# Two transformer blocks on one core: the factors for the down projection are made one by one between the next pair's products

## The chip, the core and the metric

The kernel runs on one core of a Trainium2 chip. The metric is the device time of one execution in microseconds (us). The time before is 2848.76 us, the median of 3 runs (2841.24 to 2850.15). The profile and the trace are from one further execution.

The engines are named as in the profile: PE is the matrix engine (PEld its weight loads), DVE the vector engine, ACT the scalar engine, POOL GpSimd, SP the engine that issues most loads. ACTq and SPq are the queues on which ACT and SP issue transfers.

## The reference, cut to what matters

The program runs two transformer blocks, one after the other, on 1024 tokens of width 1024. Each is a mixer (attention and others, not touched here) and a feed-forward part with 2816 hidden units:

```python
# block 1
gu = x @ w_gu                            # 1024x1024 @ 1024x5632
gate, up = gu[:, :2816], gu[:, 2816:]
ffn = (silu(gate) * up) @ w_down         # 1024x2816 @ 2816x1024
x = layer_norm(ALPHA * x + ffn, ln2_g, ln2_b)
# block 2: its six modulation rows depend on c alone
mod = silu(c) @ w_cond + b_cond          # 1x1024 @ 1024x6144
...
h = rmsnorm(x, g_ffn_pre) * (1 + scale_f) + shift_f
f = (silu(h @ w_gate) * (h @ w_up)) @ w_down
x = x + gate_f * rmsnorm(f, g_ffn_post)
```

All of it is float32. The kernel writes each factor of a matrix product as a high part (a cast to fp32r, in which PE takes it) and a low part (the rest), and makes three matmuls of each: high by high, high by low, low by high (`mm3`, L97 to L99).

## The kernel before, in words

The feed-forward part is the class `Ffn`, used once in each block (FFN1 and FFN2). Its first half, `gate_up`, has 22 tiles of 128 hidden units. Tiles 0 to 3 go through `direct`: 48 matmuls for the gate and 48 for the up part of one tile and one half of the tokens. Tiles 4 to 21 go in nine pairs p = 2 to 10. For a pair, gate and up are each a product of a 2x2 block matrix made with seven block products in place of eight (a Strassen scheme of Winograd's kind, class `Matrix`). Each block product is 12 matmuls of 128x512. The seven come in the order 1, 6, 2, 7, 5, 4, 3, first all of the gate, then all of the up part. The trace names a product by its right factor:

| product q | 1 | 6 | 2 | 7 | 5 | 4 | 3 |
|---|---|---|---|---|---|---|---|
| right factor | B11 | T2 | B21 | T3 | T1 | B12 | B22 |
| line of its eviction | 958 | 963 | 983/992 | 966 | 968 | 971 | 976 |

The weights of a product are one of four raw blocks or one of four sums of them (tile `tt`, DVE, L925). Their high part is an ACT cast (tile `wst`, L945); the low part is made on DVE, or on POOL for products 2 and 4 (L946). The results of a pair are four 128x512 blocks; the up part multiplies into the gate's on DVE (L992) or on POOL (L994).

When a pair is done, `forms` makes the left factors that the down projection will need: A11, S3, S2, A22, S1, A12, S4 for the pairs 0 to 8 (four of them are sums or differences made on DVE, L1042 to L1051). The pairs 9 and 10 have four plain stores each. `store` casts a factor on ACT (tile `hf`, L80), makes its low part on DVE (L84) and remembers it; the next `store` first issues what is remembered, from ACT's own queue (L1023), to DRAM (`h_d`, `hl_d`). `hf` and `wst` are slots of one tag, `w`, of which there are six: a cast into a slot that held an `hf` waits until its store has landed.

During FFN1's nine pairs `cond_steps` computes block 2's modulation rows: 48 loads of 512 KB (`raw_c`, three slots of the tag `raw`), each with one DVE operation on 128x1024 (L1250, L1252), and at the end of each of the six rows a split (L1264), two matmuls and a copy. One step is asked for after every second product (`extra1`). FFN2 has no such steps.

The program's text does not fix the order on the engines alone. A scheduler places each instruction by its dependencies and its priority; what stands in a `with soon():` block gets a high one. Each engine then takes its instructions strictly in the order that results.

Of the kernel before, what the change touches and what calls it, by code (L numbers as in the profile page):

```python
# [9 lines left out]
F32 = mybir.dt.float32  # L10
F32R = mybir.dt.float32r
# [12 lines left out]
P = 128  # L24
NB = S // P
KT = D // P
# [12 lines left out]
def two_blocks(ctx: ExitStack, tc: tile.TileContext, a):  # L39
# [16 lines left out]
    def slot(tag, shape, dtype, name):  # L56
        return strm.tile(shape, dtype, tag=tag, bufs=SLOTS[tag], name=name)
# [16 lines left out]
    def soon():  # L74
        return tc.high_priority(offset=4000)


    def split(hi, lo, src, hi_eng="act", lo_eng="dve"):
        if hi_eng == "act":
            A.copy(hi, src)  # L80
        else:
            V.tensor_copy(hi, src)
        eng = V if lo_eng == "dve" else G
        eng.tensor_tensor(lo, src, hi.bitcast(F32), op=OP.subtract)  # L84

    def load_split(src, shape, hi_eng="act", lo_eng="dve", alloc=slot):
        r = slot("raw", shape, F32, "raw")
        DMA.dma_start(r, src)
        h = alloc("w", shape, F32R, "wh")
        l = alloc("w", shape, F32R, "wl")  # L90
        with soon():
            split(h, l, r, hi_eng, lo_eng)
        return h, l
# [367 lines left out]
    for n, blk in enumerate(SCORED):  # L461
        if n % 4 == 0:
            iqt = p1.tile([P, 4, 256], F32, tag="qk", bufs=6, name="iq")
        o = gemm_tm(wiq, blk, 256)
# [134 lines left out]
    class LaneC:  # L599
# [7 lines left out]
        def load(self, j):  # L607
            return [load_qk(p1, 6, qk_d[4 + j], s) for s in range(2)]
# [168 lines left out]
    class SAct:  # L777
# [20 lines left out]
        def next(self):  # L798
            self.n += 1
            return self.ring[(self.n - 1) % len(self.ring)]  # L800
# [195 lines left out]
    class Ffn:  # L996
# [18 lines left out]
            DMA.dma_start(r, src)  # L1015
            return r

        def post(self, nm):
            return self.pp.tile([P, 512], F32, tag="post", bufs=12, name=nm)

        def flush(self):
            for dst, src in self.stores:
# [3 lines left out]
        def store(self, dst, x):  # L1026

            self.flush()
            t = slot("w", [P, 2, 512], F32R, "hf")
            split(t[:, 0], t[:, 1], x)  # L1030
            self.stores.append((dst, t.bitcast(F32)))

        def forms(self, i, b):

            if i >= NPAIR:
                for (j, th), x in b.items():
                    self.store(hl_d[2 * (i - NPAIR) + j][:, :, th * 512:(th + 1) * 512], x)
                return
            a11, a12, a21, a22 = b[0, 0], b[1, 0], b[0, 1], b[1, 1]
            put = lambda n, x: self.store(h_d[i][n], x)  # L1040
            s1 = self.post("s1")
            V.tensor_tensor(s1, a21, a22, op=OP.add)  # L1042
            put("A11", a11)
            V.tensor_tensor(a21, a11, a21, op=OP.subtract)  # L1044
            put("S3", a21)
            V.tensor_tensor(a11, s1, a11, op=OP.subtract)
            put("S2", a11)
            put("A22", a22)
            put("S1", s1)
            put("A12", a12)  # L1050
            V.tensor_tensor(a12, a12, a11, op=OP.subtract)  # L1051
            put("S4", a12)

        def gate_up(self, wg, wu, late, extra=None):


            act = self.act

            def direct(f, th, g, u):
                pg = ps_lg()  # L1060
                for n, (wh, wl) in enumerate((g, u)):
                    for k in range(KT):
                        mm3(pg[:, n, :], wh[:, k, :], wl[:, k, :], act.at(0, k, th), act.at(1, k, th), k == 0, k == KT - 1)
                s = self.post("silu")
                with soon():
                    A.activation(s, pg[:, 0, :], AF.Silu)
                    V.tensor_tensor(s, s, pg[:, 1, :], op=OP.mult)
                return s

            def load_gu(f):  # L1070
                return load_split(wg(f), [P, KT, P]), load_split(wu(f), [P, KT, P])

            wt = [self.w0, load_gu(1)]
            b = {}
            for th in range(2):
                for f in range(2):
                    b[f, th] = direct(f, th, *wt[f])
                    if th == 0:
                        late(4 + 2 * f)
                        late(5 + 2 * f)  # L1080
            self.forms(0, b)
            b = {}
            for f in (2, 3):
                wt = load_gu(f)
                for th in range(2):
                    b[f - 2, th] = direct(f, th, *wt)
            act.sums()
            self.forms(1, b)
            for p in range(2, NFT // 2):
                f = 2 * p  # L1090
                ms = {}
                for m in range(2):
                    w = (wg, wu)[m]
                    ms[m] = (Gate, Up)[m]([self.load(w(f + i), [P, KT, P]) for i in range(2)], act, self.post)
                    if m == 1:
                        ms[1].gate = ms[0]
                    for q in (1, 6, 2, 7, 5, 4, 3):
                        ms[m].product(q)
                        if extra is not None:
                            extra()  # L1100
                self.forms(p, {(i, l): ms[0].p[i, l] for i in range(2) for l in range(2)})
            self.flush()

        def down(self, wd, res=None):
# [138 lines left out]
    def cond_steps(j):  # L1243

        m = fpool.tile([P, D], F32, tag="rows", bufs=1, name="mod")
        for k in range(KT):
            r = slot("raw", [P, D], F32, "raw_c")
            DMA.dma_start(r, a["w_cond_2"][k * P:(k + 1) * P, j * D:(j + 1) * D])
            if k == 0:
                V.tensor_scalar_mul(m, r, sc[:, 0:1])  # L1250
            else:
                V.scalar_tensor_tensor(m, r, sc[:, k:k + 1], m, op0=OP.mult, op1=OP.add)  # L1252
            yield

        b = slot("raw", [P, D], F32, "raw_b")
        DMA.dma_start(b[0:1, :], a["b_cond_2"][j * D:(j + 1) * D].partition_broadcast(1))
        V.tensor_tensor(m[0:1, :], m[0:1, :], b[0:1, :], op=OP.add)
        gn = {1: "g_mix_pre_2", 2: "g_mix_post_2", 4: "g_ffn_pre_2", 5: "g_ffn_post_2"}.get(j)
        if gn is not None:
            g = row(slot("raw", [P, D], F32, "raw_g"), a[gn])  # L1260
        for c in range(2):
            cs = slice(c * 512, (c + 1) * 512)
            t = slot("raw", [P, 2, 512], F32, "raw_m").bitcast(F32R)
            split(t[:, 0, :], t[:, 1, :], m[:, cs])  # L1264
            o = ps_mm(512)
            T.matmul(o, ones, t[:, 0, :], start=True, stop=False)
            T.matmul(o, ones, t[:, 1, :], start=False, stop=True)
            V.tensor_copy(m[:, cs], o)
            yield
        if gn is not None:  # L1270
            V.scalar_tensor_tensor(m, m, 1.0 if j in (1, 4) else 0.0, g, op0=OP.add, op1=OP.mult)
        DMA.dma_start(mod_d[j:j + 1, :], m[0:1, :])
# [471 lines left out]
```

## Time and profile before

| what | value |
|---|---|
| median of 3 runs | 2848.76 us |
| the profiled execution | 2853.76 us; span 2852.0 us |
| PE busy | 2413.8 us (85%), 11584 matmuls |
| DVE, ACT, POOL busy | 1848.8 (65%), 1104.1 (39%), 780.3 us (27%) |
| mean granted clock of PE | 0.927 |
| FFN1 `gate_up`, the pairs | 784.4 to 1279.3 us |
| FFN2 `gate_up`, the pairs | 2140.1 to 2620.7 us |

The span is the time from the first to the last instruction in the trace; the profiled execution took 1.8 us more. A granted clock of 1.00 is 2.4 GHz, 0.50 is 1.2 GHz; a value between them over a stretch is a mean of the two. In the stretch from 2140 to 2620 us PE alternates between about 38 us of products and one idle time of about 10 us for each pair.

### The profile page before, as it was taken

The page shows a single profiled execution, that of the slowest core. Times are in us where ns is not written, and L with a number is a line of the kernel's source. Part 1 is how long each engine was busy: PE and PEld are TensorE (multiplying, and loading weights), DVE is VectorE, ACT ScalarE, POOL GpSimd, SP SyncE. Part 2 cuts the span into 40 slices and gives each one's busy share as a digit, 9 for nine tenths or more (in the row PEclk, how much of TensorE's full clock was granted, in tenths as well). Part 3 has the DMA queues.
Part 4 walks back from the last instruction along what each step waited for, and adds up shares of the span by engine and source line. Part 5 has one row for each costly group of instructions (what it writes and reads, how often), then busy time and mean ns, then how long its engine had stood idle before and what let it go on. Part 6 is the DMA issues. An engine that isn't in the chain of part 4 may idle for free. (4 is left out here: it accounts for less than half of the span.)

```text
span 2852.0 us, 33007 instructions
## 1 busy us (share of the span) xinstructions
PE 2413.8 (85%) x11584; PEld 1982.8 (70%) x11584; DVE 1848.8 (65%) x3042; ACT 1104.1 (39%) x2013; POOL 780.3 (27%) x751
## 2 busy tenths in 40 slices
PE   8889997997688667889997988898768877878998
PEld 8878876876566556668876777677556655666886
DVE  4889787457557677658775366667635546545776
ACT  4558854332232232223235244456523223224321
POOL 1511234147111111120043044337611111112004
PEclk9999998998899888999998999999788998999999
DMA  4244545422434454467633424635123223226663
GB/s 167 71 131 126 148 119 169 126 83 81 151 129 155 141 189 159 162 249 266 240 124 122 148 88 142 199 93 188 67 101 120 96 89 140 90 95 230 243 235 133
DMA packets 171726, 414.02 MB, mean 145 GB/s; under 512 B 21788, under 2 KB 67868, under 8 KB 170536
## 3 DMA queue, kind: packets, MB, share of 16 engines
q1 hardware_dynamic: 149064, 337.45, 36.3%
q10 hardware_dynamic: 22496, 74.46, 6.6%
q8 instruction: 92, 1.51, 0.2%
q14 instruction: 74, 0.61, 0.1%
HBM read 278.65 MB, written 133.19 MB: 144 GB/s over the span
## 5 line engine op out<-in xcount | busy, mean ns | idle before, releaser
L946 POOL TENSOR_TENSOR wst<-rw,wst 128x512 fp32r<-128x512 f32 x57 | 83.7, 1468 | 384.8 <-ACT wst L945 363.3
L946 DVE TENSOR_TENSOR wst<-tt,wst 128x512 fp32r<-128x512 f32 x144 | 106.9, 743 | 94.6 <-ACT wst L945 94.5
L84 POOL TENSOR_TENSOR wl<-raw,wh 128x1024 fp32r<-128x1024 f32 (+2 forms) x28 | 66.3, 2374 | 309.0 <-ACT wh L80 251.9
L945 ACT CAST wst<-tt 128x512 fp32r<-128x512 f32 x144 | 89.3, 620 | 154.9 <-PE plg L99 111.2
L337 PE MATMUL plg<-qk,qk 128*128 128x384 f32 (+4 forms) x480 | 124.7, 377 | 27.9 <-DVE mn L350 12.9
L994 POOL TENSOR_TENSOR u<-u,u 128x512 f32<-128x512 f32 x36 | 50.7, 1408 | 261.0 <-DVE u L968 212.1
L1545 DVE TENSOR_TENSOR_SCAN sab<-sab 128x640 f32<-128x640 f32 (+7 forms) x64 | 102.7, 1609 | 20.9 <-ACT sab L1543 20.2
L97 PE MATMUL pmm<-x1B11h,wst 128*128 128x512 f32 x72 | 35.0, 486 | 93.4 <-ACT wst L945 93.4
L278 ACT ACTIVATE junk_a<-xi,cand 128x1024 bf16<-128x1024 f32 (+1 forms) x124 | 109.0, 879 | 12.4 <-DVE cand L267 6.9
L97 PE MATMUL pmm<-x3B11h,wst 128*128 128x512 f32 x72 | 36.3, 504 | 90.9 <-ACT wst L945 90.9
L337 PEld LDWEIGHTS plg<-qk,qk 128*128 128x128 f32 x480 | 81.9, 198 | 38.4 <-DVE mn L350 16.5
L80 ACT CAST hf<-u 128x512 fp32r<-128x512 f32 x36 | 22.1, 615 | 189.7 <-DVE u L1044 150.2
L162 PE MATMUL pmm<-wh,xh 128*128 128x256 f32 (+1 forms) x320 | 92.2, 289 | 1.4 <-DVE stgl L399 0.8
L80 ACT CAST ws<-st 128x512 fp32r<-128x512 f32 x72 | 45.0, 628 | 123.6 <-PE plg L99 77.1
L1171 DVE TENSOR_TENSOR dacc<-dacc,plg 128x1024 f32<-128x1024 f32 x48 | 58.6, 1220 | 52.6 <-PE plg L99 52.6
L163 PE MATMUL pmm<-wl,xh 128*128 128x256 f32 (+1 forms) x320 | 91.7, 287 | 0.0
L164 PE MATMUL pmm<-wh,xl 128*128 128x256 f32 (+1 forms) x320 | 91.4, 286 | 0.0
L351 ACT ACTIVATE e<-e,mn 128x128 f32<-128x128 f32 (+7 forms) x96 | 74.2, 773 | 36.2 <-DVE mn L350 35.1
L97 PEld LDWEIGHTS pmm<-x1B11h,wst 128*128 128x128 f32 x72 | 16.8, 233 | 101.2 <-ACT wst L945 97.3
L97 PEld LDWEIGHTS pmm<-x3B11h,wst 128*128 128x128 f32 x72 | 17.4, 241 | 98.8 <-ACT wst L945 94.8
L97 PE MATMUL pmm<-xh,wh 128*128 128x512 f32 x192 | 79.0, 412 | 7.5 <-DVE oB L585 4.9
L692 PE MATMUL pmm<-woh,mixh 128*128 128x512 f32 x192 | 79.0, 411 | 4.8 <-ACT mixh L681 2.7
(733 smaller groups left out, 8607.6 us busy)
## 6 DMA issues: line engine op xcount, KB each, us to landing
raw_c<-in_w_cond_dram SPq DMA_DIRECT2D x48, 512.0 KB, 4.2
qk<-qkd SPq DMA_DIRECT2D x72, 256.0 KB, 6.7
rw<-in_wgu_dram SPq DMA_DIRECT2D x36, 512.0 KB, 3.4
rw<-in_w_down_dram SPq DMA_DIRECT2D x26, 512.0 KB, 5.5
x_d<-acc SPq DMA_DIRECT2D x24, 512.0 KB, 2.8
qk<-qk2d SPq DMA_DIRECT2D x48, 256.0 KB, 4.8
raw<-in_wqk_dram SPq DMA_DIRECT2D x20, 512.0 KB, 4.1
raw<-in_w_down_dram SPq DMA_DIRECT2D x18, 512.0 KB, 4.4
```

Of the source, the lines that this page charges most:

```text
L80: A.copy(hi, src)
L97: T.matmul(out, lh, rh, start=start, stop=False, skip_group_check=more)
L162: T.matmul(o, at(0, k, tb * P, P), h[:, j, :], start=(k == 0), stop=False)
L163: T.matmul(o, at(0, k, tb * P, P), l[:, j, :], start=False, stop=False)
L164: T.matmul(o, at(1, k, tb * P, P), h[:, j, :], start=False, stop=(k == KT - 1))
L278: A.activation(junk_a[:, :L], xi[self.blks[i]], AF.Sign, bias=c, accum_out=self.cnt[:, i:i + 1])
L337: T.matmul(pl[:, c, :n], q[:, isl], k2[:, c * n:(c + 1) * n], start=(j == 0), stop=last)
L351: A.activation(e[:, :L], e[:, :L], AF.Exp, scale=-1.0, bias=mn, accum_out=l)
L692: T.matmul(o, mh[:, k, :], wh[:, dsl], start=(k == 0), stop=False)
L945: A.copy(wh, x)
L946: (G if p in (2, 4) else V).tensor_tensor(wl, x, wh.bitcast(F32), op=OP.subtract)
L1545: V.tensor_tensor_scan(sa[:, ::-1], sa[:, ::-1], sa[:, ::-1], 1.0, op0=OP.mult, op1=OP.bypass)
```

## The change

`forms` becomes a generator: it makes one factor and yields. `gate_up` asks for one factor after each product of the next pair, until there are none left. The split of a factor gets the high priority of `soon()`. In the direct part the weights for the tiles 2 and 3 are asked for earlier, and the first pair's factors are made in the two calls of `direct(3, ...)`. The high and low parts of a modulation row (`m`) move from a `raw` slot to two tiles of the tag `post` (12 slots of 2 KB a partition, `Ffn.post`).

```diff
     def store(self, dst, x):
         self.flush()
         t = slot("w", [P, 2, 512], F32R, "hf")
-        split(t[:, 0], t[:, 1], x)
+        with soon():
+            split(t[:, 0], t[:, 1], x)
         self.stores.append((dst, t.bitcast(F32)))
     def forms(self, i, b):
...
         s1 = self.post("s1")
         V.tensor_tensor(s1, a21, a22, op=OP.add)
         put("A11", a11)
+        yield
         V.tensor_tensor(a21, a11, a21, op=OP.subtract)
         put("S3", a21)
+        yield
...
     def gate_up(self, wg, wu, late, extra=None):
...
-        def load_gu(f):
-            return load_split(wg(f), [P, KT, P]), load_split(wu(f), [P, KT, P])
-        wt = [self.w0, load_gu(1)]
+        def load(w, f):
+            return load_split(w(f), [P, KT, P])
+        wt = [self.w0, [load(wg, 1), load(wu, 1)], [load(wg, 2)], []]
...
-        self.forms(0, b)
+        todo = self.forms(0, b)
+        wt[2].append(load(wu, 2))
+        wt[3].append(load(wg, 3))
         b = {}
-        for f in (2, 3):
-            wt = load_gu(f)
-            for th in range(2):
-                b[f - 2, th] = direct(f, th, *wt)
+        for th in range(2):
+            b[0, th] = direct(2, th, *wt[2])
+        wt[3].append(load(wu, 3))
+        for th in range(2):
+            for _ in range(4):
+                next(todo, None)
+            b[1, th] = direct(3, th, *wt[3])
         act.sums()
-        self.forms(1, b)
+        todo = self.forms(1, b)
         for p in range(2, NFT // 2):
...
                 for q in (1, 6, 2, 7, 5, 4, 3):
                     ms[m].product(q)
+                    next(todo, None)
                     if extra is not None:
                         extra()
-            self.forms(p, {(i, l): ms[0].p[i, l] for i in range(2) for l in range(2)})
+            todo = self.forms(p, {(i, l): ms[0].p[i, l] for i in range(2) for l in range(2)})
+        for _ in todo:
+            pass
         self.flush()
...
     def cond_steps(j):
...
-            t = slot("raw", [P, 2, 512], F32, "raw_m").bitcast(F32R)
-            split(t[:, 0, :], t[:, 1, :], m[:, cs])
+            hl = [ffn1.post(f"m{i}", F32R) for i in "hl"]
+            split(*hl, m[:, cs])
```

ACT in FFN2, at the end of the pair whose factors are `h_d4`. `hf` are casts of factors, `wst` of weights; A11 has gone before these rows. Before:

```order
L80 CAST hf<-u_18035 128x512
L80 CAST hf<-s_18052 128x512
L80 CAST hf<-u_18072 128x512
L80 CAST hf<-s_18260 128x512
L80 CAST hf<-p_18013 128x512
L1023 DMA h_d4S_6143<-hf 128x1024
L1023 DMA h_d4S_6144<-hf 128x1024
L1023 DMA h_d4A_6145<-hf 128x1024
L1023 DMA h_d4S_6146<-hf 128x1024
L1023 DMA h_d4A_6147<-hf 128x1024
L80 CAST hf<-p_18013 128x512
L945 CAST wst<-raw 128x512
```

The same place of the change:

```order
L80 CAST hf<-u_18020 128x512
L945 CAST wst<-raw 128x512
L80 CAST hf<-s_18042 128x512
L945 CAST wst<-tt 128x512
L80 CAST hf<-u_18067 128x512
L945 CAST wst<-tt 128x512
L1023 DMA h_d4S_6143<-hf 128x1024
L1023 DMA h_d4S_6144<-hf 128x1024
L1023 DMA h_d4A_6145<-hf 128x1024
L80 CAST hf<-s_18294 128x512
L1023 DMA h_d4S_6146<-hf 128x1024
L945 CAST wst<-rw 128x512
```

Between the last product of a pair and the next cast of weights stood six casts of factors and five stores; now one cast stands there (S3, from `u_18020`), and the rest alternates with the weights of the products that follow.

PE at the same place: the last product of the up part (B22) and what comes next. Before:

```order
L99 MATMUL plg<-x3B22h,wst 128x512
L97 MATMUL pmm<-x3B11h,wst 128x512
L98 MATMUL pmm<-x3B11l,wst 128x512
L97 MATMUL ptr<-x3T2h,wst 128x512
L98 MATMUL ptr<-x3T2l,wst 128x512
```

The same place of the change:

```order
L99 MATMUL plg<-x3B22h,wst 128x512
L97 MATMUL pmm<-x3B21h,wst 128x512
L98 MATMUL pmm<-x3B21l,wst 128x512
L97 MATMUL plg<-x3T3h,wst 128x512
L98 MATMUL plg<-x3T3l,wst 128x512
```

Of the next gate the first product behind B22 was B11; now it is B21, since the next gate's B11 and T2 stand ahead of the up part's last three products (T1, B12, B22).

DVE in FFN1, at the end of the third pair (945 us in the trace of before). `mod<-raw_c` are cond steps; L976 of the up part is the last eviction of the pair. Before:

```order
L1252 SCALAR_TENSOR_TENSOR mod<-raw_c,sc,mod 128x1024 x3
L971 TENSOR_TENSOR p_8239<-plg,u_8264 128x512
L1252 SCALAR_TENSOR_TENSOR mod<-raw_c,sc,mod 128x1024 x3
L976 TENSOR_TENSOR u_8264<-plg,u_8264 128x512
L1257 TENSOR_TENSOR mod<-mod,raw_b 1x1024
L1042 TENSOR_TENSOR s_8380<-u_8118,u_8158 128x512
L84 TENSOR_TENSOR raw_m<-mod,raw_m 128x512
L1044 TENSOR_TENSOR u_8118<-s_8138,u_8118 128x512
```

The same place of the change (its line 1269 is line 1252 of before, 1044 is 1042, 1047 is 1044, 1274 is 1257):

```order
L971 TENSOR_TENSOR p_8241<-plg,u_8266 128x512
L1269 SCALAR_TENSOR_TENSOR mod<-raw_c,sc,mod 128x1024 x3
L976 TENSOR_TENSOR u_8266<-plg,u_8266 128x512
L1269 SCALAR_TENSOR_TENSOR mod<-raw_c,sc,mod 128x1024 x2
L1044 TENSOR_TENSOR s_8406<-u_8093,u_8143 128x512
L963 TENSOR_TENSOR u_8432<-ptr,p_8404 128x512
L1269 SCALAR_TENSOR_TENSOR mod<-raw_c,sc,mod 128x1024
L1047 TENSOR_TENSOR u_8093<-s_8118,u_8093 128x512
```

Three cond steps have moved from ahead of the pair's last evictions to a place between L976 and the difference for S3.

## Rows read from the trace of the kernel before

**Rows 1.** Waits of PE, 640 to 2640 us: total us, times, longest.

```profile
PE pmm L97 <- ACT wst L945: 184.3, 18, 13.0
PE plg L97 <- DVE p L971: 26.0, 30, 4.7
PE plg L97 <- ACT wh L80: 22.0, 2, 11.9
PE plg L97 <- DVE u L968: 15.7, 15, 2.6
...
PE plg L97 <- ACT ws L80: 8.8, 2, 4.4
```

**Rows 2.** Windows: the two pair loops, two pairs; span, busy us, PEclk, DMA share, GB/s.

```profile
784.40:1279.30 494.90, 385.85 (x1537) 301.30 (x1537) 326.70 (x420) 142.96 (x248) 97.43 (x66) 0.90 0.47 167
2140.06:2620.70 480.64, 379.80 (x1512) 295.27 (x1512) 253.57 (x349) 136.91 (x238) 93.83 (x66) 0.91 0.32 116
2250.51:2305.38 54.87, 42.30 (x169) 32.89 (x169) 29.22 (x41) 15.64 (x28) 9.98 (x7) 0.90 0.29 106
2524.07:2572.59 48.52, 42.05 (x169) 32.70 (x169) 24.19 (x34) 13.85 (x25) 9.99 (x7) 0.96 0.23 80
```

**Rows 3.** Timeline of the end of a pair: start, us, [idle before].

```profile
2240.07 0.69 DVE L976 TENSOR_TENSOR u<-plg,u 128x512 f32<-128x512 f32 x1 [3.22 <-PE plg L99]
2240.90 1.26 POOL L994 TENSOR_TENSOR u<-u,u 128x512 f32<-128x512 f32 x1 [2.62 <-DVE u L976]
2242.20 0.69 DVE L1042 TENSOR_TENSOR s<-u,u 128x512 f32<-128x512 f32 x1 [1.44 <-POOL u L994]
...
2243.71 0.62 ACT L80 CAST hf<-u 128x512 fp32r<-128x512 f32 x1 [12.90 <-DVE u L1044]
...
2248.07 1.15 ACTq L1023 DMA_DIRECT2D h_d3A<-hf  x1
...
2249.84 0.61 ACT L945 CAST wst<-rw 128x512 fp32r<-128x512 f32 x1
...
2250.51 0.80 PE L97 MATMUL pmm<-x3B11h,wst 128*128 128x512 f32 x1 [10.48 <-ACT wst L945]
```

**Rows 4.** Windows: an idle time, and 5 us behind three of them.

```profile
2240.00:2250.50 10.50, 0.03 (x1) 0.00 (x0) 7.18 (x11) 3.97 (x8) 1.26 (x1) 0.74 0.44 178
2250.50:2256.00 5.50, 5.49 (x14) 4.38 (x15) 5.39 (x8) 2.92 (x5) 2.33 (x2) 0.57 0.89 328
2572.60:2577.60 5.00, 5.00 (x15) 4.00 (x16) 4.93 (x7) 2.22 (x4) 1.54 (x1) 0.66 0.95 339
2140.10:2145.60 5.50, 5.50 (x13) 4.34 (x14) 5.40 (x8) 2.86 (x5) 2.40 (x2) 0.50 0.88 323
```

**Rows 5.** Timeline of ACT: a store, and a cast that waits for it.

```profile
2250.70 0.33 ACTq L1023 DMA_DIRECT2D h_d3S<-hf  x1
...
2254.21 0.62 ACT L945 CAST wst<-rw 128x512 fp32r<-128x512 f32 x1 [0.65 <-DMA h_d3S<-hf]
```

**Rows 6.** Transfers issued in FFN1: KB, median us from issue to landing.

```profile
h_d5S<-hf ACTq DMA_DIRECT2D x4, 512.0 KB, 3.9
```

**Rows 7.** Timeline of PE: the first matmul of direct tile 2, FFN2.

```profile
2079.77 0.79 PE L97 MATMUL plg<-x3B11h,wh 128*128 128x512 f32 x1 [10.05 <-ACT wh L80]
```

**Rows 8.** Timeline of FFN1's third pair: cond step and eviction (DVE).

```profile
937.65 1.28 DVE L1252 SCALAR_TENSOR_TENSOR mod<-raw_c,sc,mod 128x1024 f32<-128x1024 f32 x1 [2.37 <-DMA raw_c<-in_w_cond_dram]
938.86 0.68 DVE L971 TENSOR_TENSOR p<-plg,u 128x512 f32<-128x512 f32 x1
```

**Rows 9.** Timeline of PE at the same place.

```profile
939.69 0.76 PE L97 MATMUL plg<-x1B22h,wst 128*128 128x512 f32 x1 [4.70 <-DVE p L971]
```

**Rows 10.** Timeline after the start in rows 3: low part (POOL), sum (DVE).

```profile
2254.96 1.77 POOL L946 TENSOR_TENSOR wst<-rw,wst 128x512 fp32r<-128x512 f32 x1 [1.86 <-ACT wst L945]
...
2255.61 1.66 DVE L925 TENSOR_TENSOR tt<-raw 128x512 f32<-128x512 f32 x1
```

**Rows 11.** The chain that ended last, behind FFN2's pairs: start, us, what.

```profile
2621.69 6.25 DMA hl_d<-hf
```

More of the change, by code (lines that the diff above doesn't have):

```diff
@@ L1016, in load, with post @@
             return r
-        def post(self, nm):
-            return self.pp.tile([P, 512], F32, tag="post", bufs=12, name=nm)
+        def post(self, nm, dtype=F32):
+            return self.pp.tile([P, 512], dtype, tag="post", bufs=12, name=nm)
         def flush(self):
@@ L1043, in forms @@
             put("A11", a11)
+            yield
             V.tensor_tensor(a21, a11, a21, op=OP.subtract)
             put("S3", a21)
+            yield
             V.tensor_tensor(a11, s1, a11, op=OP.subtract)
             put("S2", a11)
+            yield
             put("A22", a22)
+            yield
             put("S1", s1)
+            yield
             put("A12", a12)
+            yield
             V.tensor_tensor(a12, a12, a11, op=OP.subtract)
             put("S4", a12)
+            yield
         def gate_up(self, wg, wu, late, extra=None):
@@ L1262, in cond_steps @@
             cs = slice(c * 512, (c + 1) * 512)
-            t = slot("raw", [P, 2, 512], F32, "raw_m").bitcast(F32R)
-            split(t[:, 0, :], t[:, 1, :], m[:, cs])
+            hl = [ffn1.post(f"m{i}", F32R) for i in "hl"]
+            split(*hl, m[:, cs])
             o = ps_mm(512)
-            T.matmul(o, ones, t[:, 0, :], start=True, stop=False)
-            T.matmul(o, ones, t[:, 1, :], start=False, stop=True)
+            for i in range(2):
+                T.matmul(o, ones, hl[i], start=i == 0, stop=i == 1)
             V.tensor_copy(m[:, cs], o)
```

## The prediction

> **What bounds the kernel now.** I read the waits of PE over both feed-forward parts first, because the page has PE busy for 85% of the span and the change touches nothing outside `gate_up`. The first line is the whole case: PE waits 184.3 us, 18 times, for ACT's cast of weights (L945) [rows 1]. There are nine such waits in each FFN: one into the first pair, seven behind pairs with seven factors, one behind a pair with four stores. The longest, 13.0, is the one into the first pair. Two waits for `wh` (L80), 22.0 in all, stand ahead of direct tile 2 [rows 1].
>
> Next I read windows over the pairs. A pair of 54.87 us has PE busy for 42.30 [rows 2], so 12.6 us of it are idle. The timeline shows what the long idle time is made of [rows 3]. The product B22 ends at 2240.03 (0.04 before its eviction L976 starts). POOL's product L994 ends at 2242.16, DVE's first sum starts at 2242.20, ACT casts the first factor at 2243.71, then come five more casts and five store issues, which take up to 1.15 us each, and only at 2249.84 the cast of the next weights. PE starts 0.67 us later, after 10.48 us. ACT works through a list in which PE's weights stand last.
>
> A second cost sits behind the wait. PE's granted clock is 0.57 in the 5.5 us that follow an idle time of 10.5 us [rows 4], so they hold 2.4 us less work than at 1.00. Behind the shorter wait that ends at 2572.6 the clock is 0.66 for 5.0 us [rows 4]: 1.7 us lost.
>
> **The boundary behind a pair with seven factors (14 of them).** In the new order of ACT one factor (S3) still stands ahead of the weights for B21, which is the product that PE wants after B22. S3 is a difference of results that B22 completes. So the wait does not vanish; its chain gets shorter. From the end of B22, with the distances of [rows 3]: DVE's first sum at 2.17; the eviction L963, which now stands behind it, at 2.78; the difference for S3 from 3.39 to 4.08 (DVE operations of 0.69 that start some 0.6 apart); ACT's cast of S3 0.09 later at 4.17; the weights' cast at 4.69 (0.52 behind a cast that follows without a wait); PE 0.67 after that, at 5.4. It was 10.5. The five casts and stores that are moved go between the next three products, where ACT has room: 15.6 us of 54.9 are busy [rows 2].
>
> Other idle time in a pair: two products that follow each other in one PSUM tile wait for the eviction between them. From the waits for L968, (15.7 - 2.6) / 14 = 0.9 each [rows 1]. Before there are two and a shorter one in a pair, 2.1 (12.6 less 10.5). Of the new order I read two as well: T1 of the gate now follows T3 directly, while B12 of the up part is covered by T2 of the next gate. With 0.1 for the low part of the first weights: 1.9.
>
> New is a wait for landings. All six slots of `w` are shared, so casts behind the boundary go into slots whose stores have just been issued. Stores issued near a boundary land in about 3.5 us: one issued at 2250.70 releases a cast at 2254.21 [rows 5]. S3's store can go at about 7.4, so the cast of S1 starts at about 11; its store goes at 12.65 and lands at 16.15. The weights of the up part's B11 then let PE start at about 17.9. PE has three products ahead of that: 36 matmuls of 0.237 (54.87 less 15.0 of losses, over 168) are 8.5 us, and 5.4 + 8.5 + 2.4 + 1.0 = 17.3. That leaves 0.6 us of waiting. Each us that a landing takes longer counts twice here.
>
> Sum for one boundary. Before: 10.5 + 2.1 + 2.4 (clock) = 15.0. After: 5.4 + 1.9 + 0.6 + 2.0 (clock, between the two rows) = 9.9. Gain 5.1, and 7 x 5.1 = 35.7 in FFN2. In FFN1 stores take 3.9 us [rows 6], 0.4 more, which costs 0.8: 7 x 4.3 = 30.1. In two of FFN1's pairs the new order puts two matmuls of B11 ahead of T1, so that T1's 12 matmuls (2.8 us) cover nothing of the landing: minus 5.6.
>
> The boundary behind the first pair with four stores waits 48.52 - 42.05 - 2.1 = 4.4 now [rows 2]. One store less stands in front: about 1.0 less in each FFN. The 4.4 into the down projection [rows 1] stays.
>
> **The start of each `gate_up`.** Tile 2's weights are asked for before the factors of the first pair, so PE need not wait. That removes 11.9 us in FFN1 [rows 1] and 10.05 in FFN2 [rows 7], each with about 2.4 of low clock: 14.3 and 12.4. The weights are loaded one call of `direct` (48 x 2 matmuls, over 20 us) ahead, which is the cover; without it a load and a cast would be in the open again. The wait of 13.05 into the first pair [rows 1] had seven factors too. What stays lies between 0.7 (a cast of weights alone) and the 5.4 from above; nothing in the trace shows this place without factors, and I take 3.3, because POOL and DVE still have low parts to make there. With 2.75 of clock in FFN2 (0.50 over 5.5 us [rows 4]) and 2.4 in FFN1, less 0.9 for T1: 11.6 and 11.2.
>
> **FFN1's cond steps.** FFN1's pairs have 494.90 - 385.85 = 109.0 us of idle PE, FFN2's 100.8 [rows 2]: the cond steps cost about 8 us. They do so where a step waits for its load at the head of DVE's queue and an eviction stands behind it: a step waited 2.37 us for `raw_c`, the eviction L971 came behind it at 938.86 [rows 8], and PE stood still for 4.70 [rows 9]. In the new order three steps of such a cluster stand between L976 and the difference for S3, so in the boundary's chain itself, and the boundary no longer has 10 us to hide them in. Below, this costs nothing more (they were in the open elsewhere). Above: three clusters of some seven steps, 1.28 each and two waits of 2.37, wholly in the open, are about 40. I take three steps of 1.28 in three clusters, 11: that is what the order shows in the chain, with loads that come in time.
>
> The high and low parts of `m` in `post` tiles move no work; they free `raw` slots for weights. I cost that at nothing: twelve `post` tiles are there, and the loads it lets go earlier are not what PE waits for.
>
> **Sum.** FFN2: 35.7 + 1.0 + 12.4 + 11.6 = 60.7. FFN1: 30.1 + 1.0 + 14.3 + 11.2 - 5.6 - 11 = 40.0. Together 100.7. The profiled execution took 2853.8, so 2753; it lies 5.0 above the median of the runs shown, so **2748 us**.
>
> **Rivals.**
> *The boundary wait goes altogether.* If the next pair's weights are cast before S3, the remaining 5.4 and its clock loss of 2.0 go too: 14 x 7.4 = 104 more, 2644. For it: this is what factors beside products could do. Against it: the order of ACT has S3's cast first.
>
> *DVE and POOL in each other's way.* Beside POOL's low part (1.77 us) a sum on DVE took 1.66 us [rows 10] where other DVE operations of 512 columns take 0.69 [rows 3]. If one low part in the new chain is held by 1.1 at each of 14 boundaries: 15 more, 2763. The Trainium skill, "SBUF — State Buffer", section "SBUF: two separate sides", says that a DVE instruction with two SBUF inputs and a GpSimd instruction that reads SBUF take a shared port pair as an exclusive lock, and that the loser blocks for the whole instruction. By that rule the 1.66 is 0.69 and a wait for POOL's end, which agrees with the trace; it speaks against the change, since factors' low parts on DVE now run beside POOL's low parts of weights, and by it the time would be that of this rival.
>
> *Landings decide.* Stores are now spread, and they share the transfer engines with loads of the next weights. One landing of a store from the same queue took 6.25 in the chain that ended last [rows 11]. If all take that, it is 2 x 2.6 x 14 = 73 more: 2821. The place is ACT's queue: behind a cast that waits for a slot, the weights of the next product wait too. Against it: two rows at 3.5 and 3.9 [rows 5, 6] for stores issued close together. This is the mechanism that could make the kernel slower: the gain of 100 is gone when landings take 100 / 28 = 3.6 us longer, about 7.3, and at 8 us the time would be about 2870.
>
> *The cond clusters in the open*: 29 more than in my sum, 2777, or 2790 with a part of the contention.
>
> *The change does nothing*, because the scheduler's order brings the casts back to the same place: the orders shown speak against it.
>
> **How the numbers follow.** My forecast 0.62; contention 0.10; cond clusters 0.10; boundary gone 0.05; landings 0.09, of which 0.04 beyond the point where the gain is gone; nothing 0.04, shared between same and slower. The likeliest gives 2748. The range reaches to 2797 above (both middle rivals, and half of the landings' price). Below, 14 x 2.0 of clock that need not be lost if the shorter wait leaves the clock up: 2720; with landings below 3.5, 2712. Within 0.3% of the time before (about 8.5 us) is what a measurement of this kernel can't tell from no change. Faster 0.92, same 0.03, slower 0.05.
>
> **What would show it.** In the waits of PE: 14 waits of about 5.4 for L945, the waiting product being B21, not B11. No wait for `wh` ahead of direct tile 2; about 3 into the first pair. FFN2's pairs near 49.8 us, where they were 54.9. Waits of under 1 us for `h_d` stores on ACT, ahead of the casts of S1 and of B11's weights. In FFN1, evictions behind `raw_c` at the ends of three pairs. The prediction is wrong if the waits at the boundaries stay near 10 or fall under 2, if landings pass 5 us, or if FFN1 loses more than 20 us to the cond steps.

## The result, and the profile after

The changed kernel takes 2798.6 us (median of 4 runs, 2795.3 to 2801.4) against 2849.5 for the kernel before, measured beside it (4 runs): a ratio of 0.9827, 95% interval 0.9805 to 0.9849. The forecast was 2748, its range ended at 2797. The direction was right, about half of the gain came. The profiled execution's span fell from 2852.0 to 2796.3 us.

The waits of PE over both feed-forward parts, which answer to [rows 1]:

```profile
PE pmm L97 <- ACT wst L945: 88.7, 21, 11.6
PE plg L97 <- ACT hf L80: 28.2, 9, 4.7
PE plg L97 <- DVE p L971: 17.4, 18, 4.0
PE plg L97 <- DVE u L966: 11.6, 6, 4.7
...
PE plg L97 <- ACT ws L80: 8.8, 2, 4.4
```

The line that held 184.3 us holds 88.7. The two waits for `wh` are gone. One line is new, 28.2 us in 9 waits (seven of them in FFN2) put down to ACT's cast `hf`, and the line for L966 has grown from 1.2 us to 11.6; both stand ahead of the matmuls into `plg`.

Windows over the two pair loops and one pair of FFN2, which answer to [rows 2]:

```profile
751.47:1257.02 505.55, 407.49 (x1537) 310.00 (x1537) 329.40 (x437) 148.01 (x262) 100.98 (x70) 0.90 0.49 169
2093.59:2565.22 471.63, 392.14 (x1514) 302.26 (x1512) 251.72 (x362) 137.53 (x245) 92.16 (x69) 0.91 0.35 122
2260.02:2312.92 52.90, 43.30 (x169) 33.56 (x169) 27.55 (x41) 15.17 (x28) 9.45 (x7) 0.92 0.30 110
```

FFN2's pairs went from 480.64 to 471.63 us, FFN1's from 494.90 *up* to 505.55. PE's busy time rose by 12 us in FFN2 and 22 in FFN1 with the same matmuls: it ran at the lower clock for longer. The six middle pairs of FFN2 take 52.6 us each (2154.69 to 2470.03), before 54.8 (2195.51 to 2524.07: 10.5 us of waiting and 44.3 us of products with short waits between them); forecast were 49.8.

Where the 55.7 us of span went, by the first matmuls of each part:

| part | before | after | difference |
|---|---|---|---|
| FFN1, direct tiles | 149.2 | 120.4 | -28.8 |
| FFN1, nine pairs | 494.9 | 505.5 | +10.6 |
| FFN2, direct tiles | 139.9 | 114.7 | -25.2 |
| FFN2, nine pairs | 480.7 | 471.6 | -9.0 |
| all else | | | -3.3 |

The boundary that answers to [rows 3], in the timeline (start, duration, engine; in brackets idle time and what ended it):

```profile
2201.70 0.69 DVE L976 TENSOR_TENSOR u<-plg,u 128x512 f32<-128x512 f32 x1 [3.15 <-PE plg L99]
2202.53 1.26 POOL L994 TENSOR_TENSOR u<-u,u 128x512 f32<-128x512 f32 x1 [2.55 <-DVE u L976]
2203.83 0.69 DVE L1044 TENSOR_TENSOR s<-u,u 128x512 f32<-128x512 f32 x1 [1.44 <-POOL u L994]
2204.44 0.68 DVE L963 TENSOR_TENSOR u<-ptr,p 128x512 f32<-128x512 f32 x1
2205.04 0.68 DVE L1047 TENSOR_TENSOR u<-s,u 128x512 f32<-128x512 f32 x1
2205.75 0.62 ACT L80 CAST hf<-u 128x512 fp32r<-128x512 f32 x1 [15.67 <-DVE u L1047]
...
2206.28 0.61 ACT L945 CAST wst<-rw 128x512 fp32r<-128x512 f32 x1
...
2206.94 0.80 PE L97 MATMUL pmm<-x3B21h,wst 128*128 128x512 f32 x1 [5.28 <-ACT wst L945]
```

From the end of B22 at 2201.66: L976, POOL, DVE's sum at 2.17, the eviction L963 at 2.78, the difference at 3.38, ACT's casts at 4.09 and 4.62, PE after 5.28. The forecast chain was 2.17, 2.78, 3.39, 4.17, 4.69 and 5.4. All seven such boundaries of FFN2 wait 5.28 or 5.29. This part was right to about a tenth.

What was not in the sum in this size stands 11 us later:

```profile
2208.88 0.33 ACTq L1023 DMA_DIRECT2D h_d3S<-hf  x1
...
2213.93 0.62 ACT L945 CAST wst<-rw 128x512 fp32r<-128x512 f32 x1 [2.86 <-DMA h_d3S<-hf]
...
2214.95 0.61 ACT L80 CAST hf<-p 128x512 fp32r<-128x512 f32 x1
...
2215.59 0.88 DVE L84 TENSOR_TENSOR hf<-p,hf 128x512 fp32r<-128x512 f32 x1 [3.13 <-ACT hf L80]
...
2216.39 0.68 DVE L946 TENSOR_TENSOR wst<-tt,wst 128x512 fp32r<-128x512 f32 x1
...
2216.99 0.68 DVE L1059 TENSOR_TENSOR p<-p,s 128x512 f32<-128x512 f32 x1
2217.59 0.68 DVE L966 TENSOR_TENSOR u<-plg,u 128x512 f32<-128x512 f32 x1
...
2218.42 0.47 PE L97 MATMUL plg<-x3T1h,wst 128*128 128x512 f32 x1 [2.76 <-ACT hf L80]
```

Read from the last row back. PE waits 2.76 us ahead of T1 for the eviction L966; T3 had ended at 2215.66. L966 starts only at 2217.59, because DVE has three instructions ahead of it, the first of them the low part of A12 (L84). That one waits for ACT's cast of A12 at 2214.95, and ACT had stood for 2.86 us before it, waiting to cast weights into a slot whose store (`h_d3S`) had not landed. By its time that store is S2's, issued at 2208.88: 5.05 us from issue to release, where [rows 5] had 3.5. ACT waits 2.6 to 2.9 us for a landing at this cast in all seven boundaries of FFN2. The page's label "ACT hf" on 28.2 us is this chain; its longest link is the landing.

PE's clock in the same pair, by windows:

```profile
2206.94:2212.00 5.06, 5.06 (x12) 3.65 (x13) 4.71 (x8) 2.65 (x5) 1.28 (x1) 0.50 0.75 222
2212.00:2215.66 3.66, 3.66 (x14) 2.64 (x12) 0.53 (x2) 1.73 (x4) 1.03 (x1) 0.86 0.99 404
2218.42:2224.00 5.58, 5.58 (x18) 4.40 (x19) 3.63 (x6) 2.31 (x5) 0.62 (x1) 0.69 0.57 231
2224.00:2250.00 26.00, 26.00 (x113) 21.01 (x112) 11.51 (x16) 6.21 (x12) 3.71 (x3) 1.00 0.18 61
```

Behind the 5.28 us of idle time the clock is 0.50 for 5.06 us and 0.86 for another 3.66 (2.5 + 0.5 us lost), and behind the second wait 0.69 for 5.58 (1.7 lost): 4.7 us, where one wait of 10.5 had cost 2.4 [rows 4].

This pair is one of the dearer ones. The same sum (length of a stretch times what its clock lacks to 1.00) over windows of 7 to 8.7 us behind each of FFN2's seven boundaries, in order:

| waits | us of work lost behind each | mean |
|---|---|---|
| before, 10.5 us | 2.6, 2.4, 2.2, 2.2, 2.2, 2.1, 2.1 | 2.2 |
| the change, 5.28 us | 1.9, 3.1, 2.1, 2.9, 2.0, 2.9, 2.9 | 2.6 |
| the change, second wait, 2.6 to 3.5 us | 1.7, 1.7, 1.5, 1.7, 1.5, 0, 1.7 | 1.4 |

So a pair loses 4.0 us to the clock in the mean, where it lost 2.2. PE's busy time over the six middle pairs says the same in a smaller size: 43.5 us a pair for 42.2.

In FFN1 the third pair's end has the cond steps in the chain, as the order had shown. DVE there, then PE:

```profile
919.62 0.68 DVE L976 TENSOR_TENSOR u<-plg,u 128x512 f32<-128x512 f32 x1
921.06 1.73 DVE L1269 SCALAR_TENSOR_TENSOR mod<-raw_c,sc,mod 128x1024 f32<-128x1024 f32 x1 [0.76 <-DMA raw_c<-in_w_cond_dram]
923.13 1.28 DVE L1269 SCALAR_TENSOR_TENSOR mod<-raw_c,sc,mod 128x1024 f32<-128x1024 f32 x1 [0.35 <-DMA raw_c<-in_w_cond_dram]
924.34 0.68 DVE L1044 TENSOR_TENSOR s<-u,u 128x512 f32<-128x512 f32 x1
...
925.54 1.28 DVE L1269 SCALAR_TENSOR_TENSOR mod<-raw_c,sc,mod 128x1024 f32<-128x1024 f32 x1
926.73 0.68 DVE L1047 TENSOR_TENSOR u<-s,u 128x512 f32<-128x512 f32 x1
```

```profile
928.64 0.79 PE L97 MATMUL pmm<-x1B21h,wst 128*128 128x512 f32 x1 [11.61 <-ACT wst L945]
```

Three steps of 1.28 and more, two of which wait for loads, stand between L976 and the difference for S3 (L1047): 11.6 us of waiting in place of 5.3. It is the only one of FFN1's seven boundaries with such a chain: four wait 5.28 or 5.29, and two wait 3.88 for a modulation row's own matmul and 0.98 behind it.

### The profile page after: what moved, and what is told of

Same layout as the page of the kernel before. It is cut to its first block, busy times and chain, and to the rows that moved or that the text cites. A ratio compares the mean times of both kernels' runs of the same rounds, so it can differ in the third digit from the quotient of the medians.

```text
span 2796.3 us, 32919 instructions
## 1 busy us (share of the span) xinstructions
PE 2436.5 (87%) x11584; PEld 1990.3 (71%) x11584; DVE 1825.5 (65%) x3042; ACT 1099.3 (39%) x2013; POOL 778.0 (28%) x751
## 4 chain that ended last, share of the span: by engine, by line
PE 48%; DVE 9%; DMA 7%; ACT 5%; POOL 4%; issue 3%; SPq 0%; ACTq 0%; DVEq 0%; POOLq 0%
PE plg L97 8%; PE plg L98 7%; PE plg L99 7%; PE pmm L97 5%; PE pmm L99 5%; PE pmm L98 5%; PE ptr L97 2%; PE ptr L99 2%; PE ptr L98 2%; ACT hf L80 2%; DMA raw_c<-in_w_cond_dram 1%; ACT wst L945 1%; POOL u L994 1%; PE plg L337 1%; DMA hl_d<-hf 1%
## 5 line engine op out<-in xcount | busy, mean ns | idle before, releaser
L84 POOL TENSOR_TENSOR wl<-raw,wh 128x1024 fp32r<-128x1024 f32 (+2 forms) x28 | 66.3, 2373 | 304.9 <-ACT wh L80 278.5
L946 DVE TENSOR_TENSOR wst<-tt,wst 128x512 fp32r<-128x512 f32 x144 | 110.3, 767 | 36.7 <-ACT wst L945 36.5
L945 ACT CAST wst<-rw 128x512 fp32r<-128x512 f32 x86 | 53.1, 617 | 89.4 <-PE plg L99 31.3
L80 ACT CAST wh<-raw 128x1024 fp32r<-128x1024 f32 x54 | 56.6, 1049 | 67.2 <-PE pmm L98 28.8
L976 DVE TENSOR_TENSOR u<-plg,u 128x512 f32<-128x512 f32 x36 | 24.9, 691 | 86.2 <-PE plg L99 86.1
L971 DVE TENSOR_TENSOR p<-plg,u 128x512 f32<-128x512 f32 x36 | 24.8, 690 | 84.3 <-PE plg L99 84.2
```

Source lines behind the costliest of these rows:

```text
L945: A.copy(wh, x)
L946: (G if p in (2, 4) else V).tensor_tensor(wl, x, wh.bitcast(F32), op=OP.subtract)
```

## The experiments

Each run's parts, from its own trace (us; medians of 4 runs, of the runs with one profile the single time):

| run | time | FFN1 direct | FFN1 pairs | FFN2 direct | FFN2 pairs |
|---|---|---|---|---|---|
| before | 2848.8 | 149.2 | 494.9 | 139.9 | 480.7 |
| the change | 2798.6 | 120.4 | 505.5 | 114.7 | 471.6 |
| start only | 2810.5 | 120.3 | 503.5 | 115.3 | 489.0 |
| pairs only | 2822.6 | 149.0 | 491.0 | 139.3 | 465.0 |
| rows in a raw slot | 2797.0 | 120.1 | 506.7 | 114.7 | 469.3 |
| half stores | 2780.9 | 119.3 | 496.5 | 116.0 | 460.6 |
| no stores | 2761.6 | 120.5 | 481.7 | 121.1 | 449.9 |
| product 2's low part on DVE | 2781.4 | 121.2 | 498.6 | 115.1 | 457.3 |
| no cond sums | 2780.6 | 120.1 | 485.4 | 116.1 | 471.1 |
| two products later | 2735.1 | 121.7 | 472.2 | 115.4 | 437.7 |
| four products later | 2638.7 | 120.4 | 421.9 | 120.2 | 384.7 |
| beside the up part only | 2602.6 | 119.3 | 409.0 | 114.9 | 369.7 |
| the same, rows in a raw slot | 2600.2 | 120.1 | 398.9 | 118.4 | 370.1 |
| the same, cond beside the gate | 2625.8 | 121.0 | 436.4 | 115.1 | 369.6 |

My first theory (A) was that the whole gain came from the start and the one-by-one factors gave nothing net; the rival (B) that they gained and something else hid it. Two runs split the change.

**Start only.**

```diff
-                todo = self.forms(p, {...})
-            for _ in todo:
-                pass
+                for _ in self.forms(p, {...}):
+                    pass
```

> Only the start of each half is changed: weights of the direct tiles ahead, factors of the direct pairs made one by one; the factors of the pairs from the third on are made at once as before, and the modulation rows are split in a raw slot as before. Theory A (all of the gain comes from the start, the one-by-one factors later gain nothing net): the start saved about 30 us in FFN1 and 25 us in FFN2 in the trace of the change, so about 2794 us, no slower than the change itself. Theory B (the one-by-one factors gained some 35 us and a loss elsewhere hid it): about 2825 us. The seven waits of 10.5 us in each half must be back under both.

Measured: 2810.5 us, ratio to before 0.9859 (0.9838 to 0.9880). That is between the two. The start saved 28.9 and 24.6 us, but the pair loops became 8.6 and 8.3 us longer. In FFN2 all of it is in the first pair (windows over the first two):

```profile
2090.61:2154.48 63.87, 44.20 (x169) 32.65 (x168) 37.68 (x54) 19.32 (x35) 13.61 (x10) 0.88 0.33 120
2154.48:2209.49 55.01, 42.46 (x168) 33.04 (x168) 29.13 (x41) 15.63 (x28) 9.97 (x7) 0.90 0.29 105
```

The first took 55.45 us in the kernel before and held 41 operations of DVE, now 54 (in FFN1 the first pair went from 54.1 to 63.5 us). The last direct pair's factors and the pair's first weights now share ACT and DVE, and PE waits inside it. In FFN2 it waits most for L966, in FFN1 for weights of T2 (4.32):

```profile
2109.50 0.77 PE L97 MATMUL plg<-x3T1h,wst 128*128 128x512 f32 x1 [4.04 <-DVE u L966]
```

So the start is worth 20 + 16 us, not 54: part of the wait of 13 us ahead of the first pair has moved into it. Of FFN2's 8.4 us more, 7.1 are idle time of PE and 1.3 its busy time.

**Pairs only**: the direct part of before, its factors drained at once, the rest as in the change.

> Only the factors from the third pair on are made one by one (and the modulation rows split in post tiles); the direct part and the first pair stay as before. Theory A: the boundary waits fall from 10.5 to 5.3 us, but waits of 2.5 to 3.5 us ahead of T1 and a lower granted clock give it back: 2849 us, give or take 8. Theory B: about 2815 us.

Measured: 2822.6 us, 0.9912 (0.9889 to 0.9935): a gain of 26, so A's "nothing" is wrong, and so is the 35 or more of B. FFN2's pairs gain 15.7 us, FFN1's 3.9 (its profiled execution was 10 us above its median, so the parts hold less than the median shows).

**Rows in a raw slot again**: the change with the last hunk of its diff undone.

> The change, but with the high and low parts of the modulation rows in a raw slot again. Theory A (their two matmuls on PE wait for parts that stand behind the factors on ACT and DVE, about 11 us in FFN1 in all, because of where the post tiles let the scheduler put them): those waits go and the time is about 2788 us. Rival: the raw slots are then taken by the rows, loads come later and the time stays at 2799 us or rises by up to 10 us.

Measured: 2797.0 us, 0.9818 (0.9798 to 0.9838), no different from the change. The rows' matmuls wait on PE up to 3.88 us in the change, but inside boundary waits that are there anyway. The move to `post` tiles costs and gains nothing, as costed.

**No cond sums.** 42 of the 48 loads and sums left out.

> The change, but 42 of the 48 loads of the conditioning weights and their sums on DVE are left out (the modulation rows are wrong for it); the split and the matmuls of each row stay where they were. If the loads and sums are what FFN1's pairs lost against FFN2's (505.5 against 471.6 us), FFN1's pairs fall to 472 to 480 us. If it is the rows' matmuls and the split in post tiles, they stay above 495 us.

Measured: 2780.6 us (one execution); FFN1's pairs 485.4, between the two numbers expected, so 20 us of their 34 us over FFN2's are the loads and sums. The rest is not separated.

Three runs on the second wait of a pair. The first two leave out part of the result and have one execution each. **Half stores** and **no stores**:

```diff
-        h_d = ... [P, 2, 512] ...
+        h_d = ... [P, 1, 512] ...      # half stores: A.dma_start(dst, src[:, :1])
-            put = lambda n, x: self.store(h_d[i][n], x)
+            put = lambda n, x: self.store(None if i else h_d[0][n], x)   # no stores
```

> The change, but only the high half of each factor of the pairs 0 to 8 is stored (256 KB in place of 512), and the down projection reads that half for both parts: the low parts are left out of the result. The factors' casts, sums and low parts stay on ACT and DVE, in the same order around the eviction L966. Theory L (PE's new wait ahead of T1 is the landing of stores: a cast of weights waits for a slot, the cast of A12 waits behind it on ACT, its low part on DVE, and L966 behind that): the wait ahead of T1 falls from 2.5 to 3.5 us to about 0.9 in FFN2's pairs, and a pair from 52.9 to about 50 us. Rival D (three DVE operations simply stand ahead of L966): the wait stays at 2.5 us or more and the pair at 52 to 53 us.

Measured: 2780.9 us; a pair takes 51.2 us (mean of six; 52.6 in the change), the second wait 1.4 to 2.9 us, and it stands ahead of the up part's B11. Neither theory's number. Of the groups `h_d2S` to `h_d8S` five land in 2.0 us where they took 3.1 to 4.3; the other two are shown, first of the change and then of this run (KB, median us to landing). The groups `h_d2A` to `h_d8A` lie between 2.3 and 5.4, before between 3.7 and 4.9.

```profile
h_d3S<-hf ACTq DMA_DIRECT2D x4, 512.0 KB, 4.5
...
h_d6S<-hf ACTq DMA_DIRECT2D x4, 512.0 KB, 4.6
```

```profile
h_d3S<-hf ACTq DMA_DIRECT2D x4, 256.0 KB, 3.1
...
h_d6S<-hf ACTq DMA_DIRECT2D x4, 256.0 KB, 4.2
```

> The change, but the factors of the pairs 1 to 8 are not stored at all; the down projection reads pair 0's factors for all (that part of the result is left out). Casts, sums and low parts of the factors stay. Slots are free as soon as the low part is made, so no cast waits for a landing. Theory L (landings make the second wait of a pair): no wait over 1 us stands between the boundary's first product and the eviction waits, the granted clock falls only once in a pair, and an FFN2 pair takes 49 to 50.5 us instead of 52.9. Rival D (the factors' work on ACT and DVE ahead of weights and evictions makes it): a wait of 1.5 us or more stays and a pair takes over 51 us.

Measured: 2761.6 us; 49.8 us a pair, the mean of six, inside theory L's range and by chance the number that I had forecast for the change. PE at one boundary, at its second wait and at T1, and the eviction L966 there:

```profile
2187.51 0.79 PE L97 MATMUL pmm<-x3B21h,wst 128*128 128x512 f32 x1 [5.28 <-ACT wst L945]
...
2196.55 0.50 PE L97 MATMUL pmm<-x3B11h,wst 128*128 128x512 f32 x1 [1.36 <-ACT wst L945]
...
2197.86 0.50 PE L97 MATMUL plg<-x3T1h,wst 128*128 128x512 f32 x1
```

```profile
2197.12 0.68 DVE L966 TENSOR_TENSOR u<-plg,u 128x512 f32<-128x512 f32 x1
```

The second wait is 0.3 to 1.6 us, and behind it the clock stays at 1.00, as theory L has it. Behind the boundary's wait 1.6 to 3.0 us of work are lost, 2.4 in the mean, much as in the change.

The order moved as well, though, in both runs: in all seven boundaries of FFN2 between 2 and 14 matmuls of B11 and T2 stand ahead of T1, where the change has none. In the boundary shown T3 ended at 2195.19. L966 starts 1.93 us after that, exactly as in the change, and T1 after 2.67 (2.76 in the change); the moved matmuls fill the time between. So these runs show what a pair takes without landings and in the order that then results. They do not separate the landing from the order. That the landing makes the wait in the change is read from the change's own trace, where ACT stands for it.

**Product 2's low part on DVE.**

```diff
-                (G if p in (2, 4) else V).tensor_tensor(wl, ...)
+                (G if p == 4 else V).tensor_tensor(wl, ...)
```

> The change, but the low part of product 2's weights (the first behind the boundary, B21) is made on DVE and no longer on POOL. In the trace of the change a factor's low part on DVE takes 1.40 us beside it, 0.69 otherwise. Rival P (POOL and DVE in each other's way lengthen the chain to the second wait): that low part takes 0.69, the second wait of a pair gets 0.7 us or more shorter and the time falls to about 2785 us. Theory L (the landings set the second wait, whoever makes the low parts): the wait stays at 2.5 to 3.5 us, and the time at 2795 us or above, since DVE has one operation more in each product 2.

Measured: 2781.4 us, 0.9760 (0.9730 to 0.9790), 17 us faster than the change and near the rival's number. In the change a factor's low part on DVE beside POOL's low part of weights:

```profile
2207.02 1.28 POOL L946 TENSOR_TENSOR wst<-rw,wst 128x512 fp32r<-128x512 f32 x1 [3.23 <-ACT wst L945]
...
2207.45 1.40 DVE L84 TENSOR_TENSOR hf<-s,hf 128x512 fp32r<-128x512 f32 x1 [0.35 <-ACT hf L80]
```

In this run both are on DVE:

```profile
2205.60 0.69 DVE L946 TENSOR_TENSOR wst<-rw,wst 128x512 fp32r<-128x512 f32 x1
2206.20 0.68 DVE L84 TENSOR_TENSOR hf<-s,hf 128x512 fp32r<-128x512 f32 x1
```

The factor's low part is back at 0.68, and DVE is done with both before it was done with the one. The order moved here too: in four of FFN2's seven boundaries two matmuls of B11 stand ahead of T1. In the three where T1 still follows T3 directly the second wait is 0.9, 1.0 and 2.1 us, in the change 2.6 to 3.5:

```profile
2163.89 0.47 PE L97 MATMUL plg<-x3T1h,wst 128*128 128x512 f32 x1 [1.01 <-DVE u L966]
```

So the rival has a share in the second wait; how much of the 17 us is its, and how much the order's, is not separated.

**The factors later.** What is left of the boundary wait is the chain to S3, which heads ACT's queue. Three runs ask for no factor during the first two, four or all seven products of the next gate:

```diff
-                    for q in (1, 6, 2, 7, 5, 4, 3):
+                    for n, q in enumerate((1, 6, 2, 7, 5, 4, 3)):
                         ms[m].product(q)
-                        next(todo, None)
+                        if m or n > 1:        # n > 3: four later; "if m": beside the up part
+                            next(todo, None)
```

> The change, but the next pair's first two products of the gate ask for no factor, so all seven come two products later and the weights of the product behind the boundary no longer stand behind the cast of S3. Theory A (what is left of the boundary wait is the chain to S3 ahead of these weights): the 5.3 us waits go in both halves, and with them part of the low clock; 14 boundaries of 5 to 7 us, so about 2710 us. Rival (landings of stores decide, and casts of weights wait for slots wherever the factors stand): the wait moves to a later product and the time is 2785 to 2800 us.

Measured: 2735.1 us, 0.9598 (0.9582 to 0.9613): between the two, nearer to A. The wait did not go; as the rival had it, it moved to a later product, T1 (PE's waits):

```profile
PE plg L97 <- ACT wst L945: 71.9, 14, 12.1
PE pmm L97 <- ACT wst L945: 15.0, 10, 2.9
```

In FFN2 it is 5.22 us now, once in a pair; the second wait has gone, and a pair takes 47.6 us (mean of six).

> As the run in which the factors come two products later, but four products later. If the wait of 5.2 us behind the cast of S3 can be outrun by products that are ready earlier, it gets shorter in each of 14 boundaries: 2690 to 2715 us. If the wait only moves with S3, 2735 us as with two.

> All seven factors stand beside the products of the next pair's up part, so the results that S3 needs are long complete when its cast comes. If the chain from the last product to S3's cast is the wait, it goes altogether and with it the low clock behind it: 14 times 6 to 7 us less than with two products' delay, about 2645 us. If post tiles run short (a pair's four results are held for seven products longer), waits of evictions take its place: 2735 us or more.

Measured: 2638.7 us (0.9255, 0.9242 to 0.9269) and 2602.6 us (0.9124, 0.9105 to 0.9143), both below what I expected. PE's waits with the factors beside the up part, and its two pair loops:

```profile
PE pmm L97 <- ACT wst L945: 8.4, 8, 2.5
...
PE plg L97 <- DVE u L966: 8.4, 4, 4.0
...
PE ptr L97 <- ACT wst L945: 5.1, 5, 2.2
```

```profile
753.20:1162.20 409.00, 372.54 (x1538) 291.81 (x1536) 341.06 (x436) 149.54 (x261) 115.65 (x70) 0.97 0.59 205
2003.70:2373.40 369.70, 357.27 (x1514) 284.75 (x1512) 281.24 (x363) 141.71 (x246) 97.43 (x69) 0.99 0.45 157
```

184.3 us of waiting for weights [rows 1] have become 16.0 (8.4, 5.1 and 2.5 in a third line), and FFN2's pairs run at 0.99 of full clock. From the change to this run FFN2's pairs get 101.9 us shorter: 34.9 are PE's busy time, at the same matmuls (392.14 to 357.27), and 67.0 its idle time. That is twice what the rival "The boundary wait goes altogether" had priced for one half (7 x 7.4 = 52); among others the second wait and its clock go too.

> As the run with all factors beside the up part, but the modulation rows are split in a raw slot as in the kernel before. If the post tiles are what FFN1 runs short of when four results are held longer, FFN1's pairs get 5 to 15 us shorter: about 2592 us. If not, 2603 us or slightly more.

Measured: 2600.2 us, 0.9123 (0.9109 to 0.9136): FFN1's pairs are 10 us shorter in the profile, but the run that they are compared with has its profile 5.7 us above its median; the medians differ by less than the runs do. Not settled.

> As the run with all factors beside the up part, but the cond steps are asked for after each product of the gate and not after every second product: the same number in a pair, beside the products that have no factor. If DVE and ACT are what FFN1's pairs still wait for (409 us against 370 in FFN2), they get 10 to 20 us shorter: about 2590 us. If it is the loads of cond weights, which come in a closer cluster then, 2603 us or more.

Measured: 2625.8 us, 0.9206 (0.9183 to 0.9229): worse, FFN1's pairs 436.4 us. The closer cluster costs more than the free slots beside the gate give; whether by its loads or by its operations on DVE is not shown.

## Why the prediction was half right

**The boundary wait** was right: 5.28 for 5.4, B21 behind S3, as read from the order and from distances of before. It is also what the later runs remove.

**The landing term** is the one that failed: "That leaves 0.6 us of waiting", ahead of the up part's B11. The chain was followed through ACT and the slots to the weights of B11 only. In the trace it leaves ACT earlier, through A12's cast to DVE, and holds L966 and so T1, one product sooner: 2.6 to 3.5 us in FFN2, 2.95 in the mean, where the sum had 1.5 in all (0.9 as an eviction wait and these 0.6). The landing that counts was longer than the 3.5 used: 5.05 us from issue to release in the rows shown, while the medians of the groups `h_d2` to `h_d8` are 3.1 to 4.9 in FFN2 (before 2.6 to 4.8). The rival "Landings decide" had the place, ACT's queue behind a cast that waits for a slot; that each us counts twice is shown by no run. "DVE and POOL in each other's way" has a share too: S2's low part is held to 1.40 us, and with it the store that the cast waits for. The Trainium skill, "SBUF — State Buffer", section "SBUF: two separate sides", speaks of an exclusive lock that blocks the loser; the rows agree: DVE's 1.40 us ends 0.55 after POOL's 1.28.

**The clock term** failed with it, and by more: 2.2 before, 2.0 forecast, 4.0 in the mean of FFN2's seven boundaries. I had one wait behind which the clock is low; there are two. The second costs 1.4, and the first alone costs 2.6, although it is half as long as the wait of before. In sum a boundary in FFN2 gained 2.2 us in place of 5.1: 1.2 more idle time than forecast, the rest clock.

**The start** was priced at 49.5 us for both halves and gave about 37. The waits for `wh` went as forecast. "I take 3.3" for the wait into the first pair looked at the wrong place: ahead of the pair the change waits 2.3 us in FFN1 and not at all in FFN2, but in the run with the start alone the first pair of each half is 8 to 9 us longer inside. The sum also gave back all of the low clock behind that wait, though a wait stays.

**FFN1.** 14.5 us were forecast for its pairs. The runs show between 4 us gained (pairs only against before) and 2 lost (the change against start only). The 11 for "three steps of 1.28 in three clusters" came in one boundary only (three of them between L976 and L1047, 11.6 us), but the loads and sums cost 20 in the change, and the second wait and the clock come on top. How these add up to the whole 14.5 stays open.

The boundary behind the pair with four stores came as forecast, 3.36 us for 3.4, in both halves.

By terms, forecast and measured: start 49.5 and 37; FFN2's pairs 36.7 and 16 to 17; FFN1's pairs 14.5 and about 0. That makes 101 and 54, against 55.7 in the span.

**The range** does not follow from its own terms: both middle rivals and half of the landings' price are 15 + 29 + 36, which reaches 2828 and not 2797.

That one factor after each product does not take a factor off the path was seen; that a later place would do so was a rival with 0.05, "the boundary wait goes altogether". The change did not do it, but the place of one `if` does.

## What to carry to other kernels

When work is spread between the steps of a pipeline, ask of each piece when its input is ready, not only where a queue has room: a piece whose input is the last result still heads an in-order queue, whatever is interleaved behind it. Follow a wait in a shared pool of slots through every engine that the waiting instruction's queue feeds, not only to its own consumer. One long wait cut into two short ones may cost more clock than it did: here 4.0 us for 2.2. When a run leaves work out to test a cause, compare its order of instructions with the other's first: here the order moved in all three runs on the second wait.

## What the runs showed of the hardware that I had not expected

The clock granted to PE fell behind waits as short as 2.7 us here (0.76 over the 7 us behind 2.66), and behind one of 2.59 it stayed at 1.00. One and the same wait of 5.28 us cost between 1.9 and 3.1 us of work within one execution, waits of 10.5 us between 2.1 and 2.6: half the wait did not mean half the clock. In the run without stores the 5.28 us cost 1.6 to 3.0.

A low part on DVE took 1.40 us beside one on POOL and 0.68 when both were on DVE. Stores of 256 KB in place of 512 landed in 2.0 us in five of seven groups, where the whole ones took 3.1 to 4.3; in the two others they fell from 4.5 to 3.1 (`h_d3S`) and from 4.6 only to 4.2 (`h_d6S`), and why is not shown.
